# Hybrid decoder layer: the channel-major input projections as one 512-column and one 256-column product, their halves summed at eviction, and q's norm folded into the score scale

## The chip, the cores and the metric

The kernel runs on one core of one Trainium2 chip. The metric is the device time of one execution in microseconds (us). A second number is the span of the profile, from the first to the last instruction of one profiled execution. TensorE does the matrix products, VectorE and ScalarE the elementwise work, GpSimd some elementwise work and some transfers; the SyncE queue issues the weight loads.

## The reference

One decoder layer over 256 tokens of 2048 channels, all in float32: an RMS norm, one input projection whose 6432 columns feed 16 dilated-window attention heads and 16 RWKV-7 heads of width 64, one output projection with residual, a second norm, a SwiGLU part of 5632 hidden columns with residual, and a last norm.

```python
u = rms_norm(h, norm1_g[l])
proj = (u @ w_in[l]).astype(jnp.float32)
q, k, v, z = jnp.split(proj, [ATTN_WIDTH, 2 * ATTN_WIDTH, 3 * ATTN_WIDTH], axis=-1)
attn = dilated_attention(q.reshape(hd), k.reshape(hd), v.reshape(hd), rel_bias_table)
rw = rwkv7_time_mix(z, ...)
mixed = jnp.concatenate([attn, rw], axis=-1)
h = h + mixed @ w_out[l]
u = rms_norm(h, norm2_g[l])
gate, up = jnp.split(u @ w_gate_up[l], 2, axis=-1)
h = h + (jax.nn.silu(gate) * up) @ w_down[l]
return rms_norm(h, final_g)
```

In the attention the logits are q k^T times 1/8 plus a bias. In the RWKV part each row of z is first mixed with the row before it (the token shift).

## The kernel before, in words

**Products in two parts.** A float32 operand is split into a high part, rounded to the type fp32r, and a low part, the rest. A product a b is taken as high*high + low*high + high*low, all summed in PSUM. The norm's factor per token (rstd1) isn't multiplied into the input: u1 is x times the gain, and the projections' results are scaled afterwards.

**Weights.** All weight matrices are read in an order that `plan_slab` lists ahead: pieces of 512 KB (128 rows by 512 columns twice, or by 256 columns four times) into three raw buffers (`load`, L122, issued by SyncE). `make` (L134) splits a piece into two pairs of halves: ScalarE rounds the high half wh (L148), VectorE subtracts to get the low half wl (L149). There are six buffers for each half, and `take` (L158) keeps the splitting up to six halves ahead of the products that read them.

**Input projections.** Two kinds. The v columns and the small low-rank columns come out token-major (`slab`, L169: tokens on the partitions, 512 or 288 weight columns moving). All the others come out channel-major, since the later work wants channels on the partitions: `slab_T` (L183) takes 256 weight columns as two blocks of 128, which are the stationary operand, and lets the 256 tokens of the input move. For each of the 16 chunks of 128 input channels and each block it issues three products of 256 columns: wh with the input's high part (L191), wh with its low part (L192), wl with the high part (L193). The result lies in the first 256 columns of a PSUM bank; `banks` (L166) gives two banks at a time, out of two sets. There are 20 such slabs: for each half of the 16 RWKV heads two each of zk, zr and zv (`zin`, L442), and for each half of the attention heads two each of qT and kT (`att_inputs`, L806).

**Evictions.** When a slab is done, VectorE multiplies each of its two blocks by rbc1, the norm's factor laid out along the tokens, on the way out of PSUM (L449 for z, L822 for qT and kT). For z the token shift follows: one ScalarE instruction (L413) and one VectorE instruction (L414).

**Order of the work.** `run` (L228) walks through the slabs, and after each step takes up to two steps of the side work: the RWKV recurrence and the attention, which are written as generators with delays between their steps on a virtual clock. The framework in which the kernel is written then settles the order on each engine when the program is built, from its own estimate of when each instruction can start. So a change in what is issued moves other instructions too. Of the side work three things are spoken of below: `blocksum` (L476), which sums over the 64 channels of each head with two products (L487 of the high half bhh, L488 of the low half blh, which VectorE makes in L484); the scores (L842) and their scaling (L848); and the transposes of the probabilities (L868).

**After the projections** come the output projection (`slab` over w_out, products named p and o), the second norm with its transposes (L247, L252, L253), the feed-forward part and the down projection. The feed-forward part already uses the other form of product: `slab_2T` (L994) holds the input's two parts side by side in one tile (u2) and issues one product of 512 columns (L1000: wh with both parts) and one of 256 (L1001: wl with the high part, onto the first half of the bank); `add_halves` (L1004) then sums the bank's two halves, a ScalarE copy (L1005) and a VectorE addition (L1006).

Of the kernel before, what the change touches and what calls it, by code (L numbers as in the profile page):

```python
# [10 lines left out]
F32 = mybir.dt.float32  # L11
# [5 lines left out]
P = 128  # L17
# [58 lines left out]
def layer(ctx: ExitStack, tc: tile.TileContext, I, out, dbg=None, upto=99):  # L76
# [30 lines left out]
    rbc1 = const.tile([P, SEQ], F32, tag="rbc1", name="rbc1")  # L107
    DVE.memset(mhalf, -0.5)
# [74 lines left out]
    def slab_T(ps, w_ap, col):  # L183

        for kc in range(NK):
            hi, lo = take(w_ap, kc, col, 0.5)
            uh_, ul_ = ulhs(kc)
            for b in range(2):
                cb = slice(b * P, (b + 1) * P)
                o = ps[b][:, 0:SEQ]  # L190
                PE.matmul(o, hi[:, cb], uh_, start=kc == 0, stop=False)  # L191
                PE.matmul(o, hi[:, cb], ul_, start=False, stop=False)  # L192
                PE.matmul(o, lo[:, cb], uh_, start=False, stop=kc == NK - 1)  # L193
            if kc % 2:
                yield

# [87 lines left out]
    pair = lambda h, l: (lambda kc: (chunk(h, kc), chunk(l, kc)))  # L284
    ulhs = pair(uh, ul)
# [42 lines left out]
    with tc.tile_pool(name="startp", bufs=1) as st:  # L328
# [57 lines left out]
        rms_scale(rstd1, accs1)  # L386
        along_tokens(rbc1, rstd1, st)
# [45 lines left out]
    def rwkv(half):  # L433
# [8 lines left out]
        def zin(pool, tag, which, name):  # L442
            dst = pool.tile([P, 4, SEQ], F32, tag=tag, name=f"{name}_{H}")
            for q in range(2):
                ps = banks(f"{name}{H}{q}")
                yield from slab_T(ps, w_in, RB + which * RW + half * 512 + q * 256)
                z = zp.tile([P, 2, SEQ], F32, tag="ztok", name=f"z_{name}{H}{q}", bufs=2)
                for j in range(2):
                    DVE.tensor_tensor(z[:, j, :], ps[j][:, 0:SEQ], rbc1, op=ALU.mult)  # L449
# [356 lines left out]
    def att_inputs(half, Z):  # L806
        A = f"b{half}"
        for i, nm in ((2, "v"), (0, "qT"), (1, "kT")):
# [7 lines left out]
            else:  # L816
                z = Z[nm] = rp.tile([P, 4, SEQ], F32, tag=nm, name=f"{nm}{A}")
                for q in range(2):
                    ps = banks(f"{nm}{A}{q}")
                    yield from slab_T(ps, w_in, col + q * 256)  # L820
                    for j in range(2):
                        DVE.tensor_tensor(z[:, 2 * q + j, :], ps[j][:, 0:SEQ], rbc1, op=ALU.mult)  # L822

    def attention(quad, Z):
# [12 lines left out]
        for pr in range(2):  # L837
# [6 lines left out]
            for h2 in range(2):  # L844
                h = 2 * pr + h2
                rb = bias[:, h, ::-1]
                for sl, b0 in zip(blocks, (128, 0)):
                    DVE.scalar_tensor_tensor(s[:, h, sl], pts[h2][:, sl], HD ** -0.5, rb[:, b0:256],  # L848
# [270 lines left out]
```

## Time and profile before

| | |
|---|---|
| median of 3 runs | 1250.55 us (1250.11 to 1251.45) |
| profiled execution: its time | 1252.15 us |
| profiled execution: its span | 1250.2 us |
| mean granted TensorE clock | 0.996 |
| TensorE busy | 1227.6 us (98%) |
| VectorE busy | 815.4 us (65%) |
| ScalarE busy | 692.9 us (55%) |
| GpSimd busy | 63.7 us (5%) |
| HBM traffic | 177 GB/s over the span |

How to read the rows below. A row of the timeline gives start, duration, engine, line, operation, output <- inputs, the partitions by elements, and in brackets the idle time before it and what ended it. The durations of products overlap, since they are pipelined; their pace is in the starts. A row of the waits reads: engine, instruction <- what it waited for: us in total, times, longest. A row of a stretch gives busy time and number of instructions for PE, PEld (weight load), DVE (VectorE), ACT (ScalarE) and POOL (GpSimd), then the granted clock, the DMA share and GB/s. A row of a group ends with count | busy us, mean ns of one | idle time before. Buffer numbers are left out of names. The slabs of the channel-major projections lie between about 26 and 403 us.

### The profile page before, as it was taken

The numbers are of one execution on the slowest core, as the hardware profiler recorded it, in microseconds if no ns is written. First come the engines' busy times: TensorE is split into PE (matmuls) and PEld (weight loads), VectorE is DVE, ScalarE is ACT, GpSimd is POOL, SyncE is SP. The second block draws the span as 40 slices with busy tenths as digits, with TensorE's granted clock in tenths as the row PEclk, the third lists the DMA queues.
The fourth block names the chain that finished last, engine by engine and source line by source line (L and its number), as shares of the span: only waits on it lengthen the run. The fifth ranks groups of instructions, "written<-read, shape, count | busy, mean of one in ns | idle before, by whom it ended". The sixth has DMA issues, their size and how long they took to land.

```text
span 1250.2 us, 21170 instructions
## 1 busy us (share of the span) xinstructions
PE 1227.6 (98%) x7930; PEld 1065.7 (85%) x7930; DVE 815.4 (65%) x1519; ACT 692.9 (55%) x1312; POOL 63.7 (5%) x69
## 2 busy tenths in 40 slices
PE   7999999999999999999999999999999999999997
PEld 6999997888899788888888888888888888888885
DVE  5787885587946857665665666666566565555653
ACT  7755655555645756565555655555565554454443
POOL 3140000120000000000000000000000000010100
PEclk9999999999999999999999999999999999999999
DMA  8657575335563476666666666666666666666664
GB/s 236 185 151 199 153 193 139 111 113 135 157 178 106 145 226 215 180 186 190 187 191 194 187 188 193 192 187 186 197 189 187 191 193 187 195 188 193 183 201 134
DMA packets 147879, 223.24 MB, mean 179 GB/s; under 512 B 18123, under 2 KB 65489, under 8 KB 147649
## 3 DMA queue, kind: packets, MB, share of 16 engines
q1 hardware_dynamic: 132176, 211.12, 57.7%
q10 hardware_dynamic: 13920, 6.06, 2.0%
q0 software_dynamic: 1680, 4.72, 1.1%
q8 instruction: 62, 1.02, 0.3%
q14 instruction: 41, 0.33, 0.1%
HBM read 218.17 MB, written 3.69 MB: 177 GB/s over the span
## 4 chain that ended last, share of the span: by engine, by line
PE 90%; DVE 4%; DMA 3%; ACT 1%; issue 1%; SPq 0%; POOLq 0%; POOL 0%; ACTq 0%; DVEq 0%
PE up L1000 13%; PE gb L1000 7%; PE ga L1000 7%; PE up L1001 6%; PE d L178 6%; PE d L180 6%; PE d L179 6%; PE gb L1001 3%; PE ga L1001 3%; DMA wr<-in_w_in_dram 2%; PE o L179 2%; PE o L180 2%; PE o L178 2%; PE qTb L191 1%; PE zrh L191 1%; PE qTb L192 1%
## 5 line engine op out<-in xcount | busy, mean ns | idle before, releaser
L149 DVE TENSOR_TENSOR wl<-wr,wh 128x512 fp32r<-128x512 f32 (+1 forms) x792 | 549.6, 700 | 367.6 <-ACT wh L148 350.9
L148 ACT ACTIVATE wh<-wr 128x512 fp32r<-128x512 f32 (+1 forms) x792 | 492.1, 627 | 470.7 <-DVE wl L149 202.1
L1000 PE MATMUL up<-u,wh 128*128 128x512 f32 x704 | 244.6, 394 | 0.0
L1001 PE MATMUL up<-u,wl 128*128 128x256 f32 x704 | 195.0, 277 | 0.0
L1000 PEld LDWEIGHTS up<-u,wh 128*128 128x128 f32 x704 | 132.0, 188 | 30.6
L1001 PEld LDWEIGHTS up<-u,wl 128*128 128x128 f32 x704 | 132.2, 188 | 0.0
L178 PE MATMUL d<-wh,hh 128*128 128x512 f32 x336 | 131.5, 391 | 0.0
L179 PE MATMUL d<-wl,hh 128*128 128x512 f32 x336 | 131.5, 391 | 0.0
L180 PE MATMUL d<-wh,hl 128*128 128x512 f32 x336 | 131.5, 391 | 0.0
L1000 PE MATMUL gb<-u,wh 128*128 128x512 f32 x352 | 130.4, 394 | 0.0
L1000 PE MATMUL ga<-u,wh 128*128 128x512 f32 x352 | 130.1, 394 | 0.0
L1001 PE MATMUL gb<-u,wl 128*128 128x256 f32 x352 | 97.6, 277 | 0.0
L1001 PE MATMUL ga<-u,wl 128*128 128x256 f32 x352 | 97.6, 277 | 0.0
L1000 PEld LDWEIGHTS ga<-u,wh 128*128 128x128 f32 x352 | 66.0, 188 | 15.3
L1000 PEld LDWEIGHTS gb<-u,wh 128*128 128x128 f32 x352 | 66.0, 188 | 15.3
L180 PEld LDWEIGHTS d<-wh,hl 128*128 128x128 f32 x336 | 63.2, 188 | 13.8
L179 PEld LDWEIGHTS d<-wl,hh 128*128 128x128 f32 x336 | 63.2, 188 | 13.8
L178 PEld LDWEIGHTS d<-wh,hh 128*128 128x128 f32 x336 | 63.2, 188 | 13.8
L1001 PEld LDWEIGHTS gb<-u,wl 128*128 128x128 f32 x352 | 66.2, 188 | 0.0
L1001 PEld LDWEIGHTS ga<-u,wl 128*128 128x128 f32 x352 | 66.0, 188 | 0.1
L1053 POOL TENSOR_TENSOR h_sb<-h_sb,fg 128x512 f32<-128x512 f32 x6 | 9.9, 1659 | 663.0 <-ACT jd L1051 663.0
L191 PE MATMUL kTb<-u1h,wh 128*128 128x256 f32 x128 | 38.1, 298 | 0.0
(293 smaller groups left out, 2095.6 us busy)
## 6 DMA issues: line engine op xcount, KB each, us to landing
wr<-in_w_gate_up_dram SPq DMA_DIRECT2D x176, 512.0 KB, 4.3
wr<-in_w_in_dram SPq DMA_DIRECT2D x96, 512.0 KB, 3.8
wr<-in_w_down_dram SPq DMA_DIRECT2D x88, 512.0 KB, 4.5
wr<-in_w_out_dram SPq DMA_DIRECT2D x32, 512.0 KB, 4.7
wr<-in_w_in_dram SPq DMA_DIRECT2D x8, 288.0 KB, 6.1
x_sb<-in_x_dram SPq DMA_DIRECT2D x8, 256.0 KB, 6.6
biasa<-rvd ACTq DMA_DIRECT2D x4, 512.0 KB, 4.7
xs<-in_x_dram POOLq DMA_DIRECT2D x4, 512.0 KB, 6.4
```

What stands on the lines that cost most here:

```text
L148: ACT.activation(hi[:, :, :n], src, AF.Copy)
L149: DVE.tensor_tensor(lo[:, :, :n], src, hi[:, :, :n].bitcast(F32), op=ALU.subtract)
L178: PE.matmul(o, ah[:, sl], hi[:, :n], start=first, stop=False)
L179: PE.matmul(o, ah[:, sl], lo[:, :n], start=False, stop=False)
L180: PE.matmul(o, al[:, sl], hi[:, :n], start=False, stop=fin)
L191: PE.matmul(o, hi[:, cb], uh_, start=kc == 0, stop=False)
L192: PE.matmul(o, hi[:, cb], ul_, start=False, stop=False)
L1000: PE.matmul(ps[b], hi[:, cb], u, start=kc == 0, stop=False)
L1001: PE.matmul(ps[b][:, 0:SEQ], lo[:, cb], u[:, 0, :], start=False, stop=kc == NK - 1)
L1053: POOL.tensor_tensor(hs, hs, fg[:, cs], op=ALU.mult)
```

## The change

The three products per chunk and block become two. The input u1 is kept in four tiles that hold both parts of a chunk side by side (`group4`, tags uu0 to uu3, in place of uh0 to uh3 and ul0 to ul3), so that wh meets both in one product of 512 columns; wl meets the high part in one of 256. `slab_2T` and `add_halves` move up from the feed-forward part, and `slab_2T` takes the number of blocks from its banks and the step of `take` as an argument; `slab_T` is gone. At the eviction `add_halves` sums the halves into z, qT or kT, and rbc1 is multiplied in by a second VectorE instruction, from SBUF to SBUF, for z and kT. For qT it isn't: the norm's factor of a query token goes with 1/8 into rq, a column per block of 128 tokens, and the scaling of the scores multiplies by that column in place of the constant. The tiles that take the place of u1 later (the split mixed heads, the first four hidden blocks) take the joined form too. Nothing in the plan of weight loads or in the side work is edited otherwise.

```diff
+    rq = const.tile([P, 2], F32, tag="rq", name="rq")
...
-    def slab_T(ps, w_ap, col):
-
+    def slab_2T(ps, w_ap, col, both, units=1):
         for kc in range(NK):
-            hi, lo = take(w_ap, kc, col, 0.5)
-            uh_, ul_ = ulhs(kc)
-            for b in range(2):
+            hi, lo = take(w_ap, kc, col, units)
+            u = both(kc)
+            for b, o in enumerate(ps):
                 cb = slice(b * P, (b + 1) * P)
-                o = ps[b][:, 0:SEQ]
-                PE.matmul(o, hi[:, cb], uh_, start=kc == 0, stop=False)
-                PE.matmul(o, hi[:, cb], ul_, start=False, stop=False)
-                PE.matmul(o, lo[:, cb], uh_, start=False, stop=kc == NK - 1)
-            if kc % 2:
+                PE.matmul(o, hi[:, cb], u, start=kc == 0, stop=False)
+                PE.matmul(o[:, 0:SEQ], lo[:, cb], u[:, 0, :], start=False, stop=kc == NK - 1)
+            if units == 1 or kc % 2:
                 yield
+
+    def add_halves(dst, ps):
+        ACT.copy(dst, ps[:, SEQ:2 * SEQ])
+        DVE.tensor_tensor(dst, ps[:, 0:SEQ], dst, op=ALU.add)
...
-    def group4(pool, tag, name, dt=F32R):
-        return [pool.tile([P, 4, SEQ], dt, tag=f"{tag}{g}", name=f"{name}{g}") for g in range(4)]
-
-    def chunk(tiles, kc):
-        return tiles[kc // 4][:, kc % 4, :]
-
-    uh = group4(act_p, "uh", "u1h")
-    ul = group4(act_p, "ul", "u1l")
+    def group4(g, name):
+        return act_p.tile([P, 4, 2, SEQ], F32R, tag=f"uu{g}", name=f"{name}{g}")
+
+    def parts(tiles):
+        return lambda kc: tiles[kc // 4][:, kc % 4]
+
+    def pair(tiles):
+        return lambda kc: (tiles[kc // 4][:, kc % 4, 0, :], tiles[kc // 4][:, kc % 4, 1, :])
+
+    u1 = [group4(g, "u1") for g in range(4)]
...
         rms_scale(rstd1, accs1)
+        DVE.tensor_scalar(rq, rstd1, HD ** -0.5, None, op0=ALU.mult)
         along_tokens(rbc1, rstd1, st)
...
-                yield from slab_T(ps, w_in, RB + which * RW + half * 512 + q * 256)
+                yield from slab_2T(ps, w_in, RB + which * RW + half * 512 + q * 256, parts(u1), 0.5)
                 z = zp.tile([P, 2, SEQ], F32, tag="ztok", name=f"z_{name}{H}{q}", bufs=2)
                 for j in range(2):
-                    DVE.tensor_tensor(z[:, j, :], ps[j][:, 0:SEQ], rbc1, op=ALU.mult)
+                    add_halves(z[:, j, :], ps[j])
+                    DVE.tensor_tensor(z[:, j, :], z[:, j, :], rbc1, op=ALU.mult)
...
-                    yield from slab_T(ps, w_in, col + q * 256)
+                    yield from slab_2T(ps, w_in, col + q * 256, parts(u1), 0.5)
                     for j in range(2):
-                        DVE.tensor_tensor(z[:, 2 * q + j, :], ps[j][:, 0:SEQ], rbc1, op=ALU.mult)
+                        o = z[:, 2 * q + j, :]
+                        add_halves(o, ps[j])
+
+                        if nm == "kT":
+                            DVE.tensor_tensor(o, o, rbc1, op=ALU.mult)
...
-                for sl, b0 in zip(blocks, (128, 0)):
-                    DVE.scalar_tensor_tensor(s[:, h, sl], pts[h2][:, sl], HD ** -0.5, rb[:, b0:256],
+                for b, sl in enumerate(blocks):
+                    DVE.scalar_tensor_tensor(s[:, h, sl], pts[h2][:, sl], rq[:, b:b + 1], rb[:, 128 - b * P:256],
                                              op0=ALU.mult, op1=ALU.add)
...
-    mh, ml = [None] * 4, [None] * 4
+    mm = [None] * 4
...
-        mh[g] = act_p.tile([P, 4, SEQ], F32R, tag=f"uh{g}", name=f"mixh{g}")
-        ml[g] = act_p.tile([P, 4, SEQ], F32R, tag=f"ul{g}", name=f"mixl{g}")
+        mm[g] = group4(g, "mixs")
...
-        run(slab_2T(gate, w_gu, f * 512))
+        run(slab_2T(gate, w_gu, f * 512, parts(u2)))
...
+        if f < 4:
+            h2 = group4(f, "hid")
+            hh, hl = h2[:, :, 0, :], h2[:, :, 1, :]
```

More of the change, by code (lines that the diff above doesn't have):

```diff
@@ L283, in layer @@
     w_in = I["w_in"].rearrange("o k n -> (o k) n")
-    pair = lambda h, l: (lambda kc: (chunk(h, kc), chunk(l, kc)))
-    ulhs = pair(uh, ul)
+    ulhs = pair(u1)
     allk = list(range(NK))
@@ L913, in until_up @@
             yield next(core)
-    mh, ml = [None] * 4, [None] * 4
+    mm = [None] * 4
     def split_mix(g):
-        mh[g] = act_p.tile([P, 4, SEQ], F32R, tag=f"uh{g}", name=f"mixh{g}")
-        ml[g] = act_p.tile([P, 4, SEQ], F32R, tag=f"ul{g}", name=f"mixl{g}")
+        mm[g] = group4(g, "mixs")
         for h in range(2):
             o = slice(2 * h, 2 * h + 2)
-            ACT.activation(mh[g][:, o, :], mixt[g][:, o, :], AF.Copy)
-            DVE.tensor_tensor(ml[g][:, o, :], mixt[g][:, o, :], mh[g][:, o, :].bitcast(F32), op=ALU.subtract)
-    mlhs = pair(mh, ml)
+            hi, lo = mm[g][:, o, 0, :], mm[g][:, o, 1, :]
+            ACT.activation(hi, mixt[g][:, o, :], AF.Copy)
+            DVE.tensor_tensor(lo, mixt[g][:, o, :], hi.bitcast(F32), op=ALU.subtract)
+    mlhs = pair(mm)
     rw, at, done = [], [], set()
@@ L964, in layer @@
     u2 = [fp.tile([P, 4, 2, SEQ], F32R, tag=f"u2{g}", name=f"u2{g}") for g in range(4)]
-    u2p = lambda kc: u2[kc // 4][:, kc % 4]
     acc2 = fp.tile([P, 2, 4], F32, tag="acc2", name="acc2")
@@ L984, in layer @@
         for kc in range(4 * sl, 4 * sl + 4, 2):
-            split_T(lambda t, k: h_sb[:, t, k * P:(k + 1) * P], lambda k: (u2p(k)[:, 0, :], u2p(k)[:, 1, :]), kc, par[:, V_G2:V_G2 + 16], "u2")
+            split_T(lambda t, k: h_sb[:, t, k * P:(k + 1) * P], pair(u2), kc, par[:, V_G2:V_G2 + 16], "u2")
     DVE.tensor_reduce(accs, acc2, axis=AX.X, op=ALU.add)
@@ L988, in layer @@
     dump("hsb", h_sb)
-    def slab_2T(ps, w_ap, col):
-        for kc in allk:
-            hi, lo = take(w_ap, kc, col)
-            u = u2p(kc)
-            for b in range(4):
-                cb = slice(b * P, (b + 1) * P)
-                PE.matmul(ps[b], hi[:, cb], u, start=kc == 0, stop=False)
-                PE.matmul(ps[b][:, 0:SEQ], lo[:, cb], u[:, 0, :], start=False, stop=kc == NK - 1)
-            yield
-    def add_halves(dst, ps):
-        ACT.copy(dst, ps[:, SEQ:2 * SEQ])
-        DVE.tensor_tensor(dst, ps[:, 0:SEQ], dst, op=ALU.add)
     rbc = fp.tile([P, SEQ], F32, tag="rbc", name="rbc")
-    hid_h, hid_l = [], []
+    hid = []
     for f in range(NF // 4):
         gate = banks(f"ga{f}") + banks(f"gb{f}")
-        run(slab_2T(gate, w_gu, f * 512))
+        run(slab_2T(gate, w_gu, f * 512, parts(u2)))
         if f == 0:
@@ L1020, in layer @@
         upp = [opsum(f"up{f}_{b}") for b in range(4)]
-        run(slab_2T(upp, w_gu, FFN + f * 512))
-        pool, th, tl = ((act_p, f"uh{f}", f"ul{f}") if f < 4 else
-                        (act_p, f"mx{2 * f - 8}", f"mx{2 * f - 7}") if f < 6 else (fp, f"hh{f}", f"hl{f}"))
-        hh = pool.tile([P, 4, SEQ], F32R, tag=th, name=f"hh{f}")
-        hl = pool.tile([P, 4, SEQ], F32R, tag=tl, name=f"hl{f}")
-        hid_h.append(hh)
-        hid_l.append(hl)
+        run(slab_2T(upp, w_gu, FFN + f * 512, parts(u2)))
+        if f < 4:
+            h2 = group4(f, "hid")
+            hh, hl = h2[:, :, 0, :], h2[:, :, 1, :]
+        else:
+            pool, tags = ((act_p, (f"mx{2 * f - 8}", f"mx{2 * f - 7}")) if f < 6 else (fp, (f"hh{f}", f"hl{f}")))
+            hh, hl = (pool.tile([P, 4, SEQ], F32R, tag=t, name=f"{n}{f}") for t, n in zip(tags, ("hh", "hl")))
+        hid.append((hh, hl))
         for b in range(4):
@@ L1040, in layer @@
     outr = out.rearrange("o (t p) d -> p (o t) d", p=P)
-    hlhs = pair(hid_h, hid_l)
+    hlhs = lambda kc: tuple(a[:, kc % 4, :] for a in hid[kc // 4])
     def down_out(ps, sl, t, parts=1):
```

## The prediction

> **What bounds the kernel now.** First the page's head and busy shares.
> ```profile
> span 1250.2 us, 21170 instructions
> PE 1227.6 (98%) x7930; PEld 1065.7 (85%) x7930; DVE 815.4 (65%) x1519; ACT 692.9 (55%) x1312; POOL 63.7 (5%) x69
> ```
> TensorE is busy for 98% of the span, so the time is that of its queue. Next the waits of TensorE over the whole span.
> ```profile
> PE bsh L488 <- DVE blh L484: 5.0, 3, 2.8
> PE PTa L868 <- DVE sa L860: 1.3, 2, 1.0
> PE rbc L262 <- DVE rb L261: 1.1, 1, 1.1
> ```
> Of those between 28 and 440 us, where the edited projections lie, these three are all that is over 0.5 us, and none names the weights' halves (wh, wl). Then busy time by stretch (PE, PEld, DVE, ACT, POOL).
> ```profile
> 36.00:100.00 64.00, 64.00 (x513) 62.35 (x512) 55.21 (x92) 44.57 (x76) 17.81 (x9) 1.00 0.60 170
> 76.00:100.00 24.00, 24.00 (x202) 24.00 (x202) 24.00 (x40) 12.05 (x22) 11.31 (x5) 1.00 0.57 157
> 100.00:250.00 150.00, 147.75 (x1423) 134.01 (x1422) 106.11 (x217) 81.67 (x139) 9.69 (x10) 1.00 0.56 156
> 250.00:400.00 150.00, 146.01 (x1393) 130.36 (x1394) 109.57 (x234) 77.82 (x152) 10.18 (x13) 0.99 0.50 137
> ```
> TensorE is full, at a granted clock of 0.99 to 1.00. VectorE is near it only from 76 to 100 us, where it has no idle moment. So a cheaper product shortens the time, and VectorE is the one engine that could take the gain back.
>
> **The change part by part.** *The products.* On TensorE's queue, second q slab of half 0, one 128-row chunk of weights for two column blocks (qTb_0, qTb_1). Before:
> ```order
> L487 MATMUL bsh_3272<-bhh_3255,onesblk 128x512
> L191 MATMUL qTb_0_3231<-u1h_89,wh_0_3137 128x256
> L192 MATMUL qTb_0_3231<-u1l_93,wh_0_3137 128x256
> L488 MATMUL bsh_3272<-blh_3256,onesblk 128x512
> L193 MATMUL qTb_0_3231<-u1h_89,wl_0_3138 128x256
> L191 MATMUL qTb_1_3232<-u1h_89,wh_0_3137 128x256
> L192 MATMUL qTb_1_3232<-u1l_93,wh_0_3137 128x256
> L193 MATMUL qTb_1_3232<-u1h_89,wl_0_3138 128x256
> ```
> Now:
> ```order
> L494 MATMUL bsh_2896<-bhh_2883,onesblk 128x512
> L192 MATMUL qTb_0_2863<-u_90,wh_0_2781 128x512
> L193 MATMUL qTb_0_2863<-u_90,wl_0_2782 128x256
> L192 MATMUL qTb_1_2864<-u_90,wh_0_2781 128x512
> L193 MATMUL qTb_1_2864<-u_90,wl_0_2782 128x256
> L192 MATMUL qTb_0_2863<-u_90,wh_0_2781 128x512
> L193 MATMUL qTb_0_2863<-u_90,wl_0_2782 128x256
> L495 MATMUL bsh_2896<-blh_2884,onesblk 128x512
> ```
> Two 256-column products became one of 512, and the block sum's second product moved from behind two short products to behind three pairs. Their pace is in the starts: a run of 256-wide ones (34 starts), a run of 512-wide ones of the v slab right after (19), and the pair of 512 and 256 columns that the feed-forward part issues already (its 512s, 17 starts).
> ```profile
> 182.79 0.28 PE L193 MATMUL zvh<-u1h,wl 128*128 128x256 f32 x1
> 186.75 0.28 PE L193 MATMUL zvh<-u1h,wl 128*128 128x256 f32 x1
> ...
> 188.26 0.39 PE L178 MATMUL vb<-wh,u1h 128*128 128x512 f32 x1
> 192.34 0.39 PE L178 MATMUL vb<-wh,u1h 128*128 128x512 f32 x1
> ...
> 599.91 0.39 PE L1000 MATMUL ga<-u,wh 128*128 128x512 f32 x1
> 605.46 0.39 PE L1000 MATMUL ga<-u,wh 128*128 128x512 f32 x1
> ...
> L193 PE MATMUL zkh<-u1h,wl 128*128 128x256 f32 x128 | 36.3, 284 | 0.0
> ```
> 256 columns: 3.96 / 33 = 0.1200 us, three of them 0.360. 512 columns: 4.08 / 18 = 0.2267. The pair: 5.55 / 16 = 0.3469, and 0.2267 + 0.1200 = 0.3467 says the same. A triple saves 0.0131 us. There are 128 of them under each of five names (zk, zr, zv, qT, kT), 640 in all: **-8.4 us**, all on the path. The durations printed (0.28, 0.39) overlap and don't count here.
>
> The Trainium skill (TensorE: Matmul & The Clock Gate, Back-to-back issue gap) puts the gap at N/2.4 + 2.5 ns, that is, merging two matmuls saves 2.5 ns; by it the sum's first term would be 640 x 2.5 ns = 1.6 us, an estimate. The starts above show 13 ns for the same step, so the measurement decides.
>
> *rq.* One 128x2 instruction stands ahead of the copies rb, for which TensorE waits. Its nearest row is a 128x16 copy:
> ```profile
> 253.83 0.17 DVE L564 COPY pcsh<-pw_h 128x16 f32<-128x16 f32 x1
> ```
> Between 0 and 0.2; I take **+0.1**.
>
> *Evictions.* 40 blocks each get a ScalarE copy; an addition takes the place of the multiplication out of PSUM; 32 of them (24 of z, 8 of kT) get a multiplication from SBUF as well. The same instructions in the feed-forward part:
> ```profile
> L449 DVE TENSOR_TENSOR z_zkh<-zkh,rbc 128x256 f32<-128x256 f32 x8 | 3.0, 416 | 0.0
> L1005 ACT COPY hd<-up 128x256 f32<-128x256 f32 x44 | 14.0, 365 | 0.0
> L1006 DVE TENSOR_TENSOR hd<-up,hd 128x256 f32<-128x256 f32 x44 | 16.5, 416 | 0.0
> L1018 DVE TENSOR_TENSOR si<-si,rbc 128x256 f32<-128x256 f32 x44 | 17.4, 418 | 0.0
> ```
> That is 40 x 0.365 = 14.6 us on ScalarE, 0 for the exchange (416 for 416), 32 x 0.418 = 13.4 us on VectorE. The cover is the next slab's 32 pairs (11.1 us): the banks come in two sets, so a slab's banks are wanted only one slab later, and an eviction of two blocks is 2 x (0.365 + 0.416 + 0.418) = 2.4 us. Behind the copy, which now waits for the slab's last product on ScalarE, stand the high halves wh of later chunks; ScalarE is idle half the time even from 76 to 100.
>
> The cover is thinnest on VectorE from 76 to 100. The low half written at 91.00, counted off in program order, is the last of its slab, and its first product starts at 94.80:
> ```profile
> 91.00 0.68 DVE L149 TENSOR_TENSOR wl<-wr,wh 128x512 fp32r<-128x512 f32 x1
> ...
> 94.80 0.28 PE L193 MATMUL zvh<-u1h,wl 128*128 128x256 f32 x1
> ```
> A lead of 3.1 us. One eviction falls into the full stretch ahead of it, 2 x 0.418 = 0.8 us, and the faster products take about 0.4: 1.9 are left. An instruction from SBUF can also be held up while GpSimd works:
> ```profile
> 249.82 2.89 DVE L149 TENSOR_TENSOR wl<-wr,wh 128x512 fp32r<-128x512 f32 x1
> ...
> 249.31 2.85 POOL L586 TENSOR_TENSOR arh<-zr_h,pw_h 128x1024 f32<-128x1024 f32 x1
> ```
> 2.89 for 0.68, so 2.2 more. If this befalls both new multiplications, 2 x 2.2 - 1.9 = 2.5 us of wait; if neither, 0. I take **+0.4**, nearer to none.
>
> *The block sums' waits.* VectorE's queue at the same place. Before:
> ```order
> L783 SCALAR_TENSOR_TENSOR y_h_2801<-bsh_3222,y_h_2801 128x512
> L822 TENSOR_TENSOR qTb_2989<-qTb_0_2990,rbc_83 128x256
> L822 TENSOR_TENSOR qTb_2989<-qTb_1_2991,rbc_83 128x256
> L484 TENSOR_TENSOR blh_3256<-y_h_2801,bhh_3255 128x512
> L149 TENSOR_TENSOR wl_0_3242<-wr_3239,wh_0_3241 128x512
> ```
> Now:
> ```order
> L790 SCALAR_TENSOR_TENSOR y_h_2463<-bsh_2852,y_h_2463 128x512
> L199 TENSOR_TENSOR qTb_2651<-qTb_0_2652,qTb_2651 128x256
> L199 TENSOR_TENSOR qTb_2651<-qTb_1_2653,qTb_2651 128x256
> L150 TENSOR_TENSOR wl_0_2872<-wr_2869,wh_0_2871 128x512
> L491 TENSOR_TENSOR blh_2884<-y_h_2463,bhh_2883 128x512
> ```
> A low half (L149, now L150) has moved ahead of blh. These are the waits that hang on it:
> ```profile
> 249.96 0.51 PE L488 MATMUL bsh<-blh,onesblk 128*128 128x512 f32 x1 [1.60 <-DVE blh L484]
> ...
> 260.30 0.50 PE L488 MATMUL bsh<-blh,onesblk 128*128 128x512 f32 x1 [2.79 <-DVE blh L484]
> ```
> The half adds 0.68 to 2.89 us ahead of blh; TensorE comes later by 3 x 0.347 - 2 x 0.120 = 0.8. The wait changes by -0.1 to +2.1; what it grows by, the one at 260 mostly loses, since VectorE has the same work until then. I take **+0.4**, and should both waits vanish instead, -4.4.
>
> *q's scale, layouts.* The scores take a column rq in place of a constant. The nearest rows:
> ```profile
> L848 DVE SCALAR_TENSOR_TENSOR sa<-Sa,biasa 128x256 f32<-128x256 f32 x16 | 6.6, 413 | 0.0
> L253 DVE SCALAR_TENSOR_TENSOR u1l<-pt_u,par,u1h 128x256 fp32r<-128x256 f32 x16 | 7.2, 479 | 2.6 <-ACT u1h L252 2.6
> ```
> At most 0.07 us each, and the last 8 are on the path: 0 to 0.5, taken as 0. The joined tiles (u1, the split mix, four of hid) keep every count and shape: 0.
>
> Sum: -8.4 + 0.1 + 0.4 + 0.4 = -7.5. The profiled execution took 1252.15 (1.95 outside its span), so 1244.65; it stood 1.6 above the median of the runs shown, 1250.55, and against that the forecast is **1243.0**.
>
> **The rivals.** *No gain per column.* If the path from the joined tile feeds 512 columns at twice the time of 256 (2 x 0.1200), a pair costs the 0.360 of a triple, nothing is saved, and the 0.9 of the other terms remains: 1251.4. Against it stand the v slab's 512-wide products in the same stage and the feed-forward pairs from a tile of the same layout. The Trainium skill's 2.5 ns, above, is the mild form of this. 7%.
>
> *The side work keeps its own time.* Recurrence and attention run beside the slabs as a chain with latencies; the kernel's waits (bsh, PTa) show where it is late. If shorter slabs uncover half of the saving as new waits, 1250.55 - 7.5 + 4.2 = 1247.3. For it: VectorE's 13.4 us more lie in that chain; against it: those waits are now 6.3 us in some 400. 9%.
>
> *VectorE becomes the bound of the first inputs.* From 36 to 100 us five evictions bring 10 multiplications. Held up by GpSimd each time, they need 10 x (0.42 + 2.2) = 26.2 us; the idle time there is 64 - 55.2 = 8.8 and the lead 3.1, so TensorE would wait 14.3 us: 1257.3. It decides from 10 us of waits on (eight of ten). GpSimd works 17.8 us of these 64, so eight is unlikely. 4%. The Trainium skill (SBUF — State Buffer, Who interferes with whom) says that a VectorE instruction with two SBUF inputs contends with a GpSimd one that reads SBUF, and one with a single SBUF input doesn't; the 2.89 row agrees, and by it the new multiplication can be held up where the old one could not.
>
> **How the numbers follow.** The forecast's case has 80%. Its ends: 1243.0 - 4.4, rounded up to 1240 because both waits hardly vanish together, and 1243.0 + 2.1 + 1.7 + 0.5 + 0.1 = 1247.4; with the second rival, 1248. Range 1240 to 1248. A measurement of this kernel tells about 0.2%, 2.5 us: faster is below 1248.05. Faster: 80 and half of the second rival, 84; same: the first rival and the other half, 12; slower: 4.
>
> **What would show it.** Right: the runs of products from 36 to 400 us step by 0.347 a pair; TensorE's waits there stay under 8 us and name blh, not wl; the first transposes of the second norm (pt_u, u2) start about 7.5 us earlier; the stretch from there to the end keeps its length. Wrong: pairs at 0.36; waits on wl or on z between 76 and 115 us; multiplications z<-z,rbc of 2 us and more; a tail between the last kT product and the output projection that is longer by what the slabs saved.

## The result, and the profile after

The kernel got slower. Median after: 1259.45 us (1258.54 to 1260.36, 4 runs); before, beside it on the same chip: 1250.43 us (1250.11 to 1251.45, 4 runs). The ratio is 1.0058, 95% interval 1.0037 to 1.0079. The forecast was 1243.0, range 1240 to 1248. The profiled execution took 1258.91 us, 0.5 below its median, while that of before (1252.15) stood 1.7 above its own; so the two traces differ by 6.8 us where the medians differ by 9.0. Single executions that were disturbed as a whole (1339 us and more, of before too) are left out below.

The page's head and the TensorE row of after: 640 products fewer (7290 for 7930), and a longer span.
```profile
span 1257.1 us, 19986 instructions
PE 1235.0 (98%) x7290; PEld 1035.9 (82%) x7290; DVE 827.5 (66%) x1552; ACT 704.8 (56%) x1352; POOL 65.5 (5%) x69
```
The stretches of the projections, after (PE, PEld, DVE, ACT, POOL; granted clock, DMA share, GB/s):
```profile
36.00:100.00 64.00, 63.48 (x351) 53.70 (x350) 56.30 (x96) 45.59 (x83) 18.18 (x9) 1.00 0.58 169
76.00:100.00 24.00, 24.00 (x137) 20.81 (x136) 23.96 (x41) 12.47 (x25) 11.61 (x5) 1.00 0.53 154
100.00:250.00 150.00, 146.27 (x1171) 119.63 (x1170) 112.14 (x235) 87.94 (x160) 12.42 (x10) 1.00 0.56 156
250.00:400.00 150.00, 146.59 (x1194) 119.98 (x1195) 114.41 (x245) 82.77 (x166) 8.89 (x13) 0.99 0.49 140
```
VectorE is still full from 76 to 100 us, and TensorE is too: nothing waits there. TensorE's waits, after:
```profile
PE bsh L495 <- DVE blh L491: 5.5, 3, 3.7
PE PTa L879 <- DVE sa L871: 1.4, 1, 1.4
PE bsh L494 <- ACT bhh L490: 0.8, 1, 0.8
PE rbc L266 <- DVE rb L265: 0.3, 1, 0.3
```
From 36 us on that is under 8 us, naming blh and not wl, as forecast. So the loss is not in a wait. The starts of the parts tell where it is. Before, on TensorE: the first product of the output projection (p), the first transposes of the second norm (pt_u), the second pair of the first up slab, the last block of the last up slab, the first product of the down projection (d):
```profile
402.81 0.40 PE L178 MATMUL p<-wh,mixh 128*128 128x512 f32 x1
...
484.30 0.71 PE L247 MATMUL pt_u<-ident,h_sb 128*128 128x128 f32 x5
...
533.69 0.40 PE L1000 MATMUL up<-u,wh 128*128 128x512 f32 x1
...
998.92 0.40 PE L1000 MATMUL up<-u,wh 128*128 128x512 f32 x1
...
999.27 0.39 PE L178 MATMUL d<-wh,hh 128*128 128x512 f32 x1
```
After, the same five, and first, from the projections, the ends of two unbroken runs of pairs:
```profile
67.68 0.39 PE L192 MATMUL zrh<-u,wh 128*128 128x512 f32 x1
...
106.89 0.40 PE L192 MATMUL zkh<-u,wh 128*128 128x512 f32 x1
...
166.73 0.40 PE L192 MATMUL zvh<-u,wh 128*128 128x512 f32 x1
...
184.06 0.40 PE L192 MATMUL zvh<-u,wh 128*128 128x512 f32 x1
...
399.81 0.39 PE L179 MATMUL p<-wh,mixs 128*128 128x512 f32 x1
...
482.32 0.81 PE L251 MATMUL pt_u<-ident,h_sb 128*128 128x128 f32 x6
...
531.64 0.39 PE L192 MATMUL up<-u,wh 128*128 128x512 f32 x1
...
1005.81 0.40 PE L192 MATMUL up<-u,wh 128*128 128x512 f32 x1
...
1006.16 0.40 PE L179 MATMUL d<-wh,hid 128*128 128x512 f32 x1
```
The projections end 3.0 us earlier (402.81 to 399.81), the second norm begins 2.0 us earlier (484.30 to 482.32), and between the two rows of the feed-forward part, 1342 pairs apart in both traces, 465.23 us became 474.17: 8.9 us more in a part whose products and their order on TensorE are the same before and after. A pair there takes 474.17 / 1342 = 0.3533 us where it took 0.3467. From d to the end nothing moved (250.9 us in both).

One row of a stretch inside gate and up says the same. Before:
```profile
560.00:980.00 420.00, 420.00 (x2425) 367.32 (x2424) 269.05 (x496) 236.42 (x456) 0.00 (x0) 1.00 0.66 190
```
After:
```profile
560.00:980.00 420.00, 420.00 (x2379) 364.26 (x2378) 262.36 (x480) 231.41 (x442) 0.00 (x0) 1.00 0.64 187
```
TensorE is never idle in either, the granted clock is 1.00 in both, and 2379 products fit where 2425 did. This count is the reading used for all the experiments: 2425 is 0.3467 us a pair, 2379 is 0.3533.

The two runs of pairs in the projections show both paces inside one execution: 39.21 us for 111 pairs (0.3532), then 17.33 for 50 (0.3466).

The starts tell one thing more. At the slow pace the steps from pair to pair repeat every three pairs: in the changed kernel the 512-column products start at 699.82, 700.18, 700.53, 700.88, 701.24, 701.59, 701.94 and 702.30 us, that is, one step of 0.36 and two of 0.35, to the end of gate and up; the traces' nanoseconds are 361, 349 and 350. In the trace of before they mostly repeat every two pairs, 350 and 343. A chunk of weights has four blocks there, so the long step comes to each of the four blocks in turn and belongs to no one tile's place.

What differs for the feed-forward part is only where its tiles lie. The new tile rq has 8 bytes per partition and takes 32, and it comes ahead of the weights' tiles, of u1's group (actp) and of the feed-forward group (fp, with u2). Before, all of these lie 32 bytes past a multiple of 64; after, on a multiple of 64. "Place" below is this, the address modulo 64, as the built programs have it.

### The profile page after: what moved, and what is told of

The parts are those of the page before. It is cut to its first block, busy times and chain, and to the rows that moved or that the text cites. A ratio compares the mean times of both kernels' runs of the same rounds, so it can differ in the third digit from the quotient of the medians.

```text
span 1257.1 us, 19986 instructions
## 1 busy us (share of the span) xinstructions
PE 1235.0 (98%) x7290; PEld 1035.9 (82%) x7290; DVE 827.5 (66%) x1552; ACT 704.8 (56%) x1352; POOL 65.5 (5%) x69
## 4 chain that ended last, share of the span: by engine, by line
PE 91%; DVE 4%; DMA 3%; ACT 1%; issue 1%; SPq 0%; POOLq 0%; POOL 0%; ACTq 0%; DVEq 0%
PE up L192 13%; PE up L193 7%; PE ga L192 7%; PE gb L192 7%; PE d L179 6%; PE d L181 6%; PE d L180 6%; PE ga L193 3%; PE gb L193 3%; PE qTb L192 2%; PE zvh L192 2%; DMA wr<-in_w_in_dram 2%; PE kTb L192 2%; PE zrh L192 2%; PE zkh L192 2%; PE o L180 2%
## 5 line engine op out<-in xcount | busy, mean ns | idle before, releaser
L192 PE MATMUL up<-u,wh 128*128 128x512 f32 x704 | 249.3, 399 | 0.0
L193 PE MATMUL up<-u,wl 128*128 128x256 f32 x704 | 197.7, 281 | 0.0
L179 PE MATMUL d<-wh,hh 128*128 128x512 f32 x208 | 81.7, 393 | 0.0
L180 PE MATMUL d<-wl,hh 128*128 128x512 f32 x208 | 81.7, 393 | 0.0
L181 PE MATMUL d<-wh,hl 128*128 128x512 f32 x208 | 81.7, 393 | 0.0
L192 PEld LDWEIGHTS ga<-u,wh 128*128 128x128 f32 x352 | 66.1, 188 | 16.4
L192 PEld LDWEIGHTS gb<-u,wh 128*128 128x128 f32 x352 | 66.1, 188 | 16.4
L179 PE MATMUL d<-wh,hid 128*128 128x512 f32 x128 | 49.8, 389 | 0.0
L181 PE MATMUL d<-wh,hid 128*128 128x512 f32 x128 | 49.8, 389 | 0.0
L180 PE MATMUL d<-wl,hid 128*128 128x512 f32 x128 | 49.8, 389 | 0.0
L192 PE MATMUL kTb<-u,wh 128*128 128x512 f32 x128 | 48.1, 411 | 0.0
L192 PE MATMUL qTb<-u,wh 128*128 128x512 f32 x128 | 47.9, 410 | 0.0
```

The lines of the kernel that those rows point to most:

```text
L179: PE.matmul(o, ah[:, sl], hi[:, :n], start=first, stop=False)
L180: PE.matmul(o, ah[:, sl], lo[:, :n], start=False, stop=False)
L181: PE.matmul(o, al[:, sl], hi[:, :n], start=False, stop=fin)
L192: PE.matmul(o, hi[:, cb], u, start=kc == 0, stop=False)
L193: PE.matmul(o[:, 0:SEQ], lo[:, cb], u[:, 0, :], start=False, stop=kc == NK - 1)
```

## The experiments

Two theories stood first. The *address theory*: the feed-forward products are slower because their tiles lie 32 bytes further on. The *phase or pace theory*: the alternating products lock into one of two paces by what ran before them, and the place has no part in it.

**1. The changed kernel with rq in two spare columns of eps**, so that every tile lies where it did before.
```
-    eps = const.tile([P, 2], F32, tag="eps", name="eps")
+    eps = const.tile([P, 4], F32, tag="eps", name="eps")
...
-    rq = const.tile([P, 2], F32, tag="rq", name="rq")
+    rq = eps[:, 2:4]
```


> The changed kernel with rq in two spare columns of the tile eps, so that no tile of its own stands in the constants and every weight, input and feed-forward tile lies at the address it had in the kernel before (32 bytes lower than in the changed kernel); the instructions and their order are the changed kernel's. Address theory (the pairs of the feed-forward part step slower because its tiles lie 32 bytes off): their step goes back from 0.354 to 0.348 us, 1408 pairs give back 9.4 us, about 1250 us or less. Phase theory (the products fall into one of two paces by what runs before them, wherever the tiles lie): the step stays at 0.354 and the time at 1259.

Measured: 1251.16 us (1248.55 to 1253.62, 11 runs), ratio 1.0000, interval 0.9989 to 1.0010. Its stretch:
```profile
560.00:980.00 420.00, 420.00 (x2425) 367.32 (x2424) 267.94 (x491) 236.54 (x455) 0.00 (x0) 1.00 0.66 190
```
The old pace is back. So it is rq's tile, and not the products, the evictions or q's scale, that slows the feed-forward part.

**2. Kernel before with an unused tile of 32 bytes** at rq's place.
```
+    pad = const.tile([P, 8], F32, tag="pad", name="pad")
+    DVE.memset(pad, 0.0)
```


> The kernel before with an unused tile of 32 bytes a partition (and one memset of it) behind rbc1 in the constants: every later tile lies where it lies in the changed kernel, nothing else changes. Address theory: the feed-forward pairs step at 0.354, about 9.4 us more, 1260 us. Phase theory: 0.348 and 1250.5.

Measured: ratio 1.0057, interval 1.0036 to 1.0079. The executions form two groups: three at 1250.9 to 1252.4, nine at 1259.3 to 1264.4. The one profiled is of the first group:
```profile
560.00:980.00 420.00, 420.00 (x2425) 367.29 (x2424) 268.96 (x496) 236.66 (x455) 0.00 (x0) 1.00 0.65 190
```
The loss comes to the kernel before with no other edit than the tile and its one memset, as the address theory has it; but the same program can also run at the old pace, which that theory doesn't allow.

**3. and 4. The changed kernel with rq's tile of 64 bytes, and before with 64 bytes of padding**: 32 past a multiple of 64 again (the pad's width is 16 columns in both).

> The changed kernel with rq's tile padded to 64 bytes a partition, so that later tiles lie 64 bytes off the kernel before instead of 32. Address theory, if what matters is the place within 64 bytes: back to 0.348 a pair, 1250 us or less; if within 128 bytes: 0.354 or another step, about 1259. Phase theory: 0.354, 1259.

> The kernel before with an unused tile of 64 bytes a partition in the constants. Address theory within 64 bytes: 0.348, 1250.5; within 128 bytes: slower by up to 9.4 us. Phase theory: 0.348, 1250.5.

Measured: after 1249.80 us, ratio 1.0002 (0.9982 to 1.0021), eight executions at 1249.2 to 1251.5 and two at 1259.3 and 1260.0; before 1253.66, ratio 1.0013 (0.9998 to 1.0028), one of ten at 1260.4. The profiled executions, after and then before:
```profile
560.00:980.00 420.00, 420.00 (x2425) 370.35 (x2424) 268.58 (x492) 236.77 (x455) 0.00 (x0) 1.00 0.66 190
...
560.00:980.00 420.00, 420.00 (x2425) 370.31 (x2424) 269.04 (x494) 236.97 (x457) 0.00 (x0) 1.00 0.65 191
```
So it isn't that more bytes slow it; and the slow pace isn't quite excluded here either.

**5. and 6. The products grouped**: per chunk of weights first all blocks' 512-column products, then the 256-column ones; with rq in eps, and with rq's own tile.
```
             for b, o in enumerate(ps):
-                cb = slice(b * P, (b + 1) * P)
-                PE.matmul(o, hi[:, cb], u, start=kc == 0, stop=False)
-                PE.matmul(o[:, 0:SEQ], lo[:, cb], u[:, 0, :], start=False, stop=kc == NK - 1)
+                PE.matmul(o, hi[:, b * P:(b + 1) * P], u, start=kc == 0, stop=False)
+            for b, o in enumerate(ps):
+                PE.matmul(o[:, 0:SEQ], lo[:, b * P:(b + 1) * P], u[:, 0, :], start=False, stop=kc == NK - 1)
```


> The changed kernel with rq in eps's spare columns, and in slab_2T first the 512-column products of all blocks of a chunk, then the 256-column ones (two and two in the projections, four and four in the feed-forward part). Pace theory (a run of alternating 512 and 256 columns locks into 0.3467 or 0.3533 us a pair, and runs of one width have one pace, as the triples and the v slab show): every pair costs 0.3467 on average, the half of the projection pairs that stepped at 0.3533 come back, about 2 us, no execution falls 9 us behind: 1249. If grouped products have two paces as well: some stretches at 0.353 and the spread of before.

> The changed kernel itself, rq's own tile and the 32-byte shift kept, with the grouped order of products alone. Pace theory: the slow executions vanish, 1249 to 1250, where the changed kernel has 1259. Address theory (tiles at 0 of 64 bytes make the products slower in any order): 1259.

Measured: 1258.54 us, ratio 1.0052 (1.0035 to 1.0070), and 1257.46, ratio 1.0045 (1.0030 to 1.0059). The first one's stretch:
```profile
560.00:980.00 420.00, 420.00 (x2395) 366.98 (x2395) 264.05 (x489) 233.53 (x448) 0.00 (x0) 1.00 0.65 188
```
2395 products, 0.3507 us per two; with rq's own tile it is 2396. Alternation is not what costs; without it the products are slower than at the good pace, and the place no longer matters. The phase theory's expectation, that grouping removes the slow pace, failed.

**7. The changed kernel with one more 128x128 product at the head of each of the 22 feed-forward slabs**, whose result the next product overwrites.
```
+            if kc == 0 and len(ps) == 4:
+                PE.matmul(ps[0][:, 0:P], ident, ident, start=True, stop=True)
```


> The changed kernel with one extra 128x128 float32 product into the first bank at the start of each of the 22 feed-forward slabs; the slab's own first product overwrites it. Each costs about 0.25 us, 5.5 us in all. Pace theory with a lock that holds until something else runs on TensorE: the slabs draw their pace anew, some step at 0.3467 and some at 0.3533. Address theory: all at 0.3533.

Measured: one run, 1264.75 us; all slabs 22.83 us long, where 64 pairs at 0.3533 and the extra product are 22.75. In this one execution the pace isn't drawn anew at a break.

**8. The changed kernel with 96 unused bytes ahead of the fp group**: u2 goes back to 32 past a multiple of 64, the weights stay on one.
```
+    pad = fp.tile([P, 24], F32, tag="pad", name="pad")
+    DVE.memset(pad, 0.0)
```


> The changed kernel with 96 unused bytes ahead of the feed-forward part's tiles, so that the normed input u2 lies at 32 of 64 bytes as in the kernel before, while the weights' halves stay at 0 of 64. If the place of the moving operand sets the odds of the slow pace: mostly 1250. If the place of the stationary weights does: mostly 1259, as the changed kernel. If neither: either way, without order.

Measured: 1255.70 us (1254.07 to 1258.03, 11 runs), ratio 1.0033 (1.0022 to 1.0044):
```profile
560.00:980.00 420.00, 420.00 (x2403) 366.11 (x2402) 265.91 (x487) 233.60 (x449) 0.00 (x0) 1.00 0.65 188
```
A third pace: 64 pairs of a slab take 0.3500 us each.

**9. Kernel before with 32 unused bytes ahead of the fp group**: the other crossing, u2 on a multiple of 64 and the weights 32 past it. The edit is that of 8 with 8 columns.

> Kernel before with 32 unused bytes at the head of the last group of tiles (fp) only: the weights' tiles keep their place (32 past a multiple of 64 bytes), u2, the moving side of gate and up, comes to a multiple of 64. Nothing else is changed. If only one side's place decides: stationary side (weights) decides -> 0.3467 us a pair, ratio 1.000, 1251; moving side (u2) decides -> 0.353 us a pair, ratio 1.006, 1258 to 1260. If the two sides add up, the case that moved u2 alone back (0.3500) makes this one a middle pace too: 0.350 us a pair, ratio 1.003, 1254 to 1256. The phase theory (no place decides, only what ran before) has no reason for another pace than before: 1251.

Measured: 1252.03 us (1250.00 to 1256.91), ratio 1.0006 (0.9993 to 1.0019); 2426 products in the stretch. u2's place alone does nothing here.

**10. and 11. The two halves of the change apart.** The changed kernel (rq in eps) with the evictions of before, which leaves out the low half of the input; and the kernel before with the work of the new evictions added, the products untouched.
```
-                    add_halves(z[:, j, :], ps[j])
-                    DVE.tensor_tensor(z[:, j, :], z[:, j, :], rbc1, op=ALU.mult)
+                    DVE.tensor_tensor(z[:, j, :], ps[j][:, 0:SEQ], rbc1, op=ALU.mult)
```
```
-                    DVE.tensor_tensor(z[:, j, :], ps[j][:, 0:SEQ], rbc1, op=ALU.mult)
+                    ACT.copy(z[:, j, :], ps[j][:, 0:SEQ])
+                    DVE.tensor_tensor(z[:, j, :], ps[j][:, 0:SEQ], z[:, j, :], op=ALU.max)
+                    DVE.tensor_tensor(z[:, j, :], z[:, j, :], rbc1, op=ALU.mult)
```


> The changed kernel with rq's numbers in the spare columns of eps (places as before), and the new evictions taken out: one multiplication by rbc1 per result, as before. It leaves out the half of every projection that belongs to the low part of the input. What is left of the change is the products alone. If the evictions and the waits that they bring cost what the prediction says (0.8 us): 1250.3, ratio to before 0.999. If they cost the 3 to 4 us that are missing between the products' gain and the measured standing of the version with its places restored: 1247 to 1248, ratio 0.997. If the products themselves gain less than forecast, because half of the projections' pairs step at 0.3533 and not 0.3467: the projections' stretches still show both paces, and the time stays at 1250 to 1251.

> Kernel before, its products untouched, with the work of the new evictions added: a copy on ScalarE and one more operation on VectorE per result of r, k, v and k transposed, the copy alone for q. It computes the same. Prediction: +0.8 us, 1251.4 against 1250.6, ratio 1.0006 at most. If the evictions are what ate the change's gain: +3 to 4 us, ratio 1.003. Feed-forward at 0.3467 a pair by every theory.

Measured: products alone 1249.56 us against 1251.73, ratio 0.9988 (0.9973 to 1.0003), a gain of 1.5 us, between 3.4 and none; one of its twelve executions took 1258.2 us, though all places are those of before. Evictions alone 1254.78, ratio 1.0026 (1.0016 to 1.0037), 3.3 us, between 2.0 and 4.6. Both have 2425 products in the feed-forward stretch. So the two halves about cancel, as version 1 shows them together. What eats the 3.3 us is not seen in a wait: version 11's projections last 378.0 us in its trace, 1.8 more than before's 376.2, but those of version 9, in which nothing there was edited, last 377.9. Only the medians carry it.

**12. Kernel before with 96 bytes of padding at rq's place**: all later tiles on a multiple of 128.

> Kernel before with 96 unused bytes after rq's place, so that all later tiles lie at a multiple of 128 bytes (before: 32 past one; with 32 bytes of padding: 64 past; with 64 bytes: 96 past). If what counts is the place by 64 bytes: as with 32 bytes of padding, 1258 to 1260 in most executions, pairs at 0.353 us. If it is the place by 128 bytes, and a multiple of 128 is a good place: 1251, pairs at 0.3467 us. If padding as such costs (one more memset on VectorE at the start): 0.1 us.

Measured: 1260.49 us (1259.79 to 1261.59, 4 runs), ratio 1.0070 (1.0051 to 1.0088):
```profile
560.00:980.00 420.00, 420.00 (x2379) 364.33 (x2378) 262.94 (x483) 231.78 (x444) 0.00 (x0) 1.00 0.65 186
```
By 64 bytes, not by 128; and this time the trace shows before's own code at the slow pace.

**13. to 15. One kind of weights' tile moved alone** (changed kernel, rq in eps, 32-byte pads before and behind the kind): the high halves, the low halves, the raw tiles, which TensorE doesn't read. For the raw tiles:
```
+        if i == 0:
+            DVE.memset(wp.tile([P, 8], F32, tag="pad1", name="pad1"), 0.0)
         raw = wp.tile([P, 1024], F32, tag="wraw", name=f"wr{i}", bufs=RAWB)
...
+                if (i, j) == (0, 0):
+                    DVE.memset(wp.tile([P, 8], F32, tag="pad2", name="pad2"), 0.0)
                 hi = wp.tile([P, 512], F32R, tag="whi", name=f"wh{i}_{j}", bufs=SPLB)
```


> The changed kernel with all tiles where they are before the change (32 past a multiple of 64 bytes), except the weights' high halves, which lie at a multiple of 64. If the high halves, the stationary side of the 512-column products, decide: pairs in the feed-forward part at 0.3500 to 0.3533 us, ratio 1.003 to 1.006. If the low halves or the raw tiles decide: 0.3467, ratio 1.000, 1251. If any two of them must lie alike: 0.3500 here and in the next run.

> As the run before, with the low halves alone at a multiple of 64 bytes. If the low halves, the stationary side of the 256-column products, decide: 0.3500 to 0.3533 us a pair, ratio 1.003 to 1.006. If the high halves or the raw tiles decide: 0.3467, ratio 1.000, 1251.

> As the two runs before, with the raw tiles alone at a multiple of 64 bytes, which TensorE doesn't read. If TensorE's own reading of the weights decides: 0.3467 us a pair, ratio 1.000, 1251. If the transfers into the raw tiles, or the reading of them by ScalarE and VectorE, disturb the products: 0.3500 to 0.3533, ratio 1.003 to 1.006.

Measured, high halves: 1254.41 us, ratio 1.0021 (1.0010 to 1.0032). Gate and up keep the good pace, and the down projection is slower:
```profile
560.00:980.00 420.00, 420.00 (x2425) 370.35 (x2424) 268.92 (x494) 237.41 (x456) 0.00 (x0) 1.00 0.66 190
...
1010.00:1230.00 220.00, 220.00 (x945) 176.91 (x944) 118.35 (x167) 103.86 (x170) 9.85 (x6) 1.00 0.61 189
```
The kernel before in the second of these stretches:
```profile
1010.00:1230.00 220.00, 220.00 (x961) 180.45 (x960) 119.56 (x169) 105.20 (x173) 9.85 (x6) 1.00 0.62 192
```
945 products for 961, 1.7% slower, over 242 us 4.2 us; the output projection, from p to pt_u, takes 84.0 us for version 1's 82.5. Its projections never show the slow pace, and 51 products of 512 columns from 165.82 to 183.05 us step at 0.3445, the fastest pair of all. Low halves: 1258.69, ratio 1.0059 (1.0044 to 1.0074); gate and up at a fourth pace (0.3485 us per pair by the count), and the down projection 3.0 us longer:
```profile
560.00:980.00 420.00, 420.00 (x2410) 366.58 (x2409) 266.43 (x488) 234.38 (x451) 0.00 (x0) 1.00 0.66 189
```
Raw tiles: ratio 1.0037 (1.0013 to 1.0062), again two groups, four executions at 1251.0 to 1251.9 and six at 1258.7 to 1261.2; the profiled one is of the second:
```profile
560.00:980.00 420.00, 420.00 (x2379) 364.18 (x2378) 262.45 (x480) 231.65 (x442) 0.00 (x0) 1.00 0.65 187
```
TensorE's tiles lie as in version 3, which had two slow executions of ten; six of ten against two is too few to say that the raw tiles' place made the difference. None of the three reproduces the changed kernel's pace for certain.

**16. and 17. u1's group alone on a multiple of 64** (changed kernel, rq in eps; run twice). The side work's tiles, which lie behind this group, move with it.
```
+    DVE.memset(act_p.tile([P, 8], F32, tag="pad1", name="pad1"), 0.0)
     u1 = [group4(g, "u1") for g in range(4)]
...
+    DVE.memset(fp.tile([P, 8], F32, tag="pad2", name="pad2"), 0.0)
     h_sb = fp.tile([P, 2, D], F32, tag="h", name="h_sb")
```


> As the three runs before, with u1 (and what else lies in its group of tiles: the mixed input and part of the hidden values) alone at a multiple of 64 bytes. The feed-forward part reads weights and u2 in their old places: 0.3467 us a pair by every theory. If the place of the moving side sets the pace of the projections' pairs: one pace in all their stretches; if that is 0.3467, the time falls by some 3 us to 1248, ratio 0.998; if 0.3533, it rises by 1 to 2 us. If both paces still show up, what sets the pace there isn't this place: 1251.

> The same kernel as the run with u1 alone at a multiple of 64 bytes, which took 1262 to 1265 us and left no usable profile. If the place of u1 slows the pairs of the projections that read it: the projections last some 12 us longer (640 pairs at 0.365 us), the feed-forward part as before. If the pace of the feed-forward part depends on the places of tiles that its gate and up products don't read, as with the raw tiles: gate and up longer by 9 us, the projections at their two paces.

Measured: 1262.5 to 1265.2 us in all six executions, ratio 1.0099 (1.0082 to 1.0116) and 1.0098 (1.0078 to 1.0118). The projections now keep one pace, and it is the good one:
```profile
69.31 0.39 PE L192 MATMUL zrh<-u,wh 128*128 128x512 f32 x1
...
107.92 0.39 PE L192 MATMUL zkh<-u,wh 128*128 128x512 f32 x1
```
That is 38.61 us for the 111 pairs that took 39.21 in the changed kernel. But gate and up, which read nothing of this group, run at the slow pace, and the down projection, part of whose input lies in it, too; so does the output projection, whose input lies in it (84.0 us for 82.5):
```profile
560.00:980.00 420.00, 420.00 (x2379) 365.73 (x2378) 263.94 (x487) 232.39 (x448) 0.00 (x0) 1.00 0.65 186
...
1010.00:1230.00 220.00, 220.00 (x952) 178.41 (x952) 122.24 (x179) 105.82 (x178) 9.86 (x6) 1.00 0.61 189
```
That the feed-forward part keeps its old pace by every theory, as the first of the two expectations has it, failed: the places of the operands don't decide alone. The second one had this as its other case.

**18. The changed kernel without the transfers of gate's and up's weights** (the last six loads stay).
```
         w_ap, kcs, col, n, _ = plan[i]
+        if w_ap is w_gu and plan[i + 2 * RAWB][0] is w_gu:
+            raws.append(raws[-RAWB])
+            return
```


> The changed kernel, tiles where the change puts them, without the transfers of the weights of gate and up: ScalarE and VectorE split what lies in the three raw tiles from the output projection, again and again; the last six loads stay. It leaves out the weights of gate and up. If the transfers into the raw tiles set the slow pace: pairs at 0.3467 us, 1249 to 1250, ratio 0.999. If ScalarE's and VectorE's reading, or TensorE's own, sets it: 0.3533, 1258 to 1260, ratio 1.006.

Measured: 1259.50 us, ratio 1.0054 (1.0035 to 1.0074); eight of ten executions at 1258.3 to 1262.0, two at 1249.9 and 1252.5. The profiled one:
```profile
560.00:980.00 420.00, 420.00 (x2380) 364.17 (x2379) 263.75 (x484) 231.89 (x444) 0.00 (x0) 1.00 0.00 1
```
The DMA share is 0.00, and the pace is the slow one. Transfers don't make it.

**All together.** Place of each kind modulo 64, pace of gate and up in the profiled execution (slab length / 64), and how many of the executions took over 1256 us (for 8 and 13, which have a middle pace or a slower down projection, that count says little).

| version | raw | high | low | u1 group | u2 group | us a pair | above 1256 |
|---|---|---|---|---|---|---|---|
| before, all runs | 32 | 32 | 32 | 32 | 32 | 0.3467 | 0 of 117 |
| 1 rq in eps | 32 | 32 | 32 | 32 | 32 | 0.3467 | 0 of 11 |
| 3 rq of 64 bytes | 32 | 32 | 32 | 32 | 32 | 0.3467 | 2 of 10 |
| 4 before + 64 | 32 | 32 | 32 | 32 | 32 | 0.3467 | 1 of 10 |
| 10 evictions of before | 32 | 32 | 32 | 32 | 32 | 0.3467 | 1 of 12 |
| changed kernel | 0 | 0 | 0 | 0 | 0 | 0.3533 | 4 of 4 |
| 2 before + 32 | 0 | 0 | 0 | 0 | 0 | 0.3467 | 9 of 12 |
| 12 before + 96 | 0 | 0 | 0 | 0 | 0 | 0.3533 | 4 of 4 |
| 18 no transfers | 0 | 0 | 0 | 0 | 0 | 0.3533 | 8 of 10 |
| 8 fp shifted | 0 | 0 | 0 | 0 | 32 | 0.3500 | 5 of 11 |
| 9 before, fp shifted | 32 | 32 | 32 | 32 | 0 | 0.3467 | 1 of 12 |
| 13 high moved | 32 | 0 | 32 | 32 | 32 | 0.3467 | 2 of 10 |
| 14 low moved | 32 | 32 | 0 | 32 | 32 | 0.3489 | 4 of 4 |
| 15 raw moved | 0 | 32 | 32 | 32 | 32 | 0.3533 | 6 of 10 |
| 17 u1 moved (with 16) | 32 | 32 | 32 | 0 | 32 | 0.3533 | 6 of 6 |

Shown: the loss is a pace of the feed-forward products; 32 bytes in the layout bring it and taking them back removes it (with all kinds at 0, 25 of 30 executions are slow, with all at 32, 4 of 160); it is neither a wait, nor the granted clock, nor the transfers, nor, in the one execution of version 7, a phase that a break resets. Not shown: by what path the place acts. No kind of tile explains it alone, a kind that the products don't read can bring it (17), and one program can run at either pace in different executions (2, 3, 4, 10, 15, 18). What ScalarE and VectorE read and write beside the products (in 17, the first hidden blocks lie in the moved group) no run has taken out. Both theories fall in their strict form; what is left is that the place sets the odds of a pace which then holds to the end of gate and up. No version beat the kernel before by more than the measurement tells.

## Why the prediction was wrong, step by step

- **"q's scale, layouts": taken as 0.** This is the step that failed most. "The joined tiles keep every count and shape: 0" looked at counts and shapes and not at where tiles come to lie, and rq was costed as one instruction (0.1) and not as 32 bytes ahead of everything else. The term measures +8.9 us, and with it "the stretch from there to the end keeps its length" fell: 1250.2 - 484.30 = 765.9 before, 1257.1 - 482.32 = 774.8 after. No rival named it. Of the 16.4 us between 1243.0 and 1259.45 it is 8.9; the other 7.5 are the whole gain of the forecast, which version 1, with the old places, doesn't show either (1.0000). The terms below are that second step.
- **The products: -8.4.** Right in sign, too large. Counted over every step that starts at a product under the five names, whatever comes next, and without idle times, they took 239.2 us before (1920 products) and 236.0 after (1280): 3.2 saved. (Between products of the five names alone the steps add up to 226.1 and 219.8 us, but that leaves out the steps into other products, 72 before and 75 after.) A pair at 0.3467 saves the forecast 0.0131 us, one at 0.3533 half of it; of the 354 pairs in the longer unbroken runs of the changed kernel 251 have the second pace. The prediction took the feed-forward pairs' pace as the pair's one price. In version 1, with the places of before, 130 of these 354 are slow, in 13 and 17 none; so here, too, the place alone doesn't decide. A smaller part is the granted clock: after the long wait for blh it is 0.63 from 262 to 266 us before, where products of bsh and gh run, and 0.64 from 250 to 254 us after, where four of q's pairs take 0.64 us each, 1.2 us more than at the good pace. The 2.5 ns per merge of the Trainium skill (TensorE: Matmul & The Clock Gate, Back-to-back issue gap), which that section gives for an isolated product, would make 1.6 us of it, an estimate; the traces show 3.2 us / 640 = 5.0 ns on average, and 13 ns at the good pace.
- **Evictions: +0.4.** The cover held as the trace tells it: no wait on wl or z, and the new multiplications are not held up.
```profile
L456 DVE TENSOR_TENSOR z_zkh<-z_zkh,rbc 128x256 f32<-128x256 f32 x8 | 3.4, 419 | 0.1
L833 DVE TENSOR_TENSOR kTb<-kTb,rbc 128x256 f32<-128x256 f32 x8 | 3.3, 420 | 0.1
```
  Version 11's medians price them at 2.0 to 4.6 us all the same. Where these lie stays open.
- **The block sums' waits: +0.4.** The mechanism came as described: a low half ahead of blh, and GpSimd beside both. VectorE, GpSimd and TensorE in the changed kernel:
```profile
246.64 1.79 DVE L150 TENSOR_TENSOR wl<-wr,wh 128x512 fp32r<-128x512 f32 x1
248.35 2.83 DVE L491 TENSOR_TENSOR blh<-y_h,bhh 128x512 fp32r<-128x512 f32 x1
...
247.84 2.79 POOL L593 TENSOR_TENSOR arh<-zr_h,pw_h 128x1024 f32<-128x1024 f32 x1
...
251.24 0.80 PE L495 MATMUL bsh<-blh,onesblk 128*128 128x512 f32 x1 [3.74 <-DVE blh L491]
```
  The wait of 1.60 grew to 3.74, and that of 2.79 at 260 us is gone: 4.4 became 3.7. All waits on blh together went from 5.0 to 5.5 us, near the +0.4, and one of 0.8 on bhh is new. The forecast's bounds held.
- **What else of the gain went.** From the first z product to p, before 376.2 us, after 372.9: 3.3 saved. That is the products' 3.2 and 0.6 in other products, less 0.5 of new idle time (7.5 us before, 8.0 after). Of these 3.3 only 2.0 reach pt_u: the first z product starts 0.3 later (26.57 and 26.90), and the output projection takes 1.0 more (402.81 to 484.30 is 81.5 us, 399.81 to 482.32 is 82.5; version 1 has 82.5 as well, version 10, with the old evictions, 81.5). There the steps of the attention's products Sa and Oa add up to 7.2 us before and 8.5 after, without new idle time; the prediction has no term for it, and its cause stays open. The second rival (the side work keeps its own time: half of the saving comes back as waits), which had 9%, shows in the 0.5 us of idle time at most. These are single executions, and the projections of before's own code last 374.4 us in version 12 and 377.9 in version 9 without an edit there; so this point is argued and not shown.
- **The other rivals.** "No gain per column" didn't come: no run of pairs steps at 0.36. "VectorE becomes the bound" didn't come: from 76 to 100 us TensorE has no idle moment. And rq's tile isn't all: version 1, which is the change with the old places, stands at 1.0000 within 0.1%, where -7.5 us would be 0.994.

## What to carry to other kernels

Where TensorE is full, a new small tile can be an edit to every product whose tiles lie behind it, as rq was here: keep the addresses of the large tiles when a change is measured (put small values into spare columns, or pad), else the layout's effect is booked on the change. Price a product by its pace in several stretches and executions, since one kernel's alternating products can step at several paces. And look first whether a part that wasn't edited kept its length: here that one comparison told more than every wait.

## What was unexpected in the hardware

- The pair of a 512- and a 256-column product, never waiting and at a granted clock of 1.00, stepped at 0.3467, 0.3485 to 0.3489, 0.3500 or 0.3533 us in gate and up (0.3445 in the projections of version 13), by the layout and the execution, and kept its pace through 22 slabs, some 490 us. In the changed kernel the slow pace is a pattern of three pairs, 349, 350 and 361 ns.
- The same products grouped instead of alternating took 0.3507 us per two, with the tiles at either of the two places.
- Products of 512 columns in the down projection took 220 / 961 = 0.2289 us with all tiles in like places, and 220 / 945 = 0.2328 with the high halves alone moved by 32 bytes.
- VectorE's blh took 2.83 us beside GpSimd's L593, where 0.69 is its median. The Trainium skill (SBUF — State Buffer, Who interferes with whom) says that instructions with two SBUF inputs contend so; this row agrees.
